# Block 2's output projection with its operands prepared up to 28 steps ahead, and half of the first row half's transposes moved among products of the feed forward

## The chip, the cores and the metric

The kernel runs on one core of a Trainium2 chip. The metric is the device time of one launch in microseconds (us), as the median of several runs. A profile of one execution gives, for each engine, what it ran and what it waited for: TensorE (PE, and PEld for its weight loads), VectorE (DVE), ScalarE (ACT), GpSimd (POOL) and SyncE (SP), whose queue issues the transfers.

## What is computed

Two transformer blocks on one sequence of 1024 rows and 1024 columns, in float32. The first is an attention and pooling mixer. The second, in which the change lies, ends like this (cut):

```python
    merged = g_a * (o_a @ w_branch_a[l]) + g_b * (o_b @ w_branch_b[l])
    x = x + merged @ w_out[l]                              # output projection
    h2 = rms_norm(x, norm2[l])
    x = x + jnp.square(jax.nn.relu(h2 @ w_up[l])) @ w_down[l]   # feed forward, 4096 wide
return rms_norm(x, final_norm)
```

## The kernel before, in words

Every float32 operand of a matmul is split into a high part (a cast on ScalarE, `hi`, L109, to the reduced type fp32r) and a low part (operand minus high part, `lo`, L112, on VectorE or GpSimd). One product of two operands is then three matmuls: high by high, high by low, low by high. All matmuls of this part have a weight tile of 128 x 128 and 512 columns.

The output projection, the up and the down projection are multiplied by a scheme of seven products in place of eight (halves of rows, of columns and of the inner dimension are added and subtracted first). `ORDER` = 1, 6, 7, 4, 2, 5, 3 is their order in the output projection. A product of it is 48 matmuls: 4 tiles t of rows, 4 pieces q of the inner dimension, 3 matmuls each.

**Merge.** `merge` (L1487) is the stretch before: for j = 0 to 7 it multiplies by the branch weights and gathers into `gl`. From j = 4 on, `m_sums` (L1476) forms on VectorE the sums of the merged halves that the projection needs (tiles `ms` and `gl`).

**Operands of the projection.** The object `FO` of class `Feed` holds a list of 72 steps, written by `row_steps` (L845): differences of weight tiles on VectorE (`comb`, L834: tiles `cb` and `wr`, L838) and splits (`split`, L812: a cast `fh`; its low part `fl` is issued with the next step; of 14 low parts 5 go to VectorE, 9 to GpSimd). Product 1 needs the first 8 steps, product 6 the next 20, product 7 another 8, product 4 another 12, products 2, 5 and 3 8 each. A step is issued in one of two ways. `Stream.tick` issues one whenever the program's own clock `e.t` (a sum of model costs over the matmuls issued so far) has moved on by `gap` and the position lies below a goal; `need` issues at once what a product wants and sets the goal `ahead` steps further. `merge` sets the goal by `FO.ahead(8 * (j - 5))`, `row_prod` (L873) by its argument 16. `F` is the same kind of object for the up projection.

**Order of other work.** `e.at(dt, fn)` puts work on a heap, due `dt` ns of program time later. Each engine runs its own instructions strictly in the order in which the program issued them, so these dues decide who stands behind whom.

**Rows.** When a tile of a product is complete, `out2_gather` (L1551) adds it to the residual row tile (`x`, L1554, VectorE). For the last four products it also takes the sum of squares (`junk`, L404, ScalarE); when both column halves are there, `f3` adds them on GpSimd (L1563), takes the inverse root there (`ry`, L117 and L118), scales the row on VectorE (`xs`, two of 512 columns, L1567) and stores `x`. Rows t = 0 to 3 are finished by product 3, rows 4 to 7 by product 5. Only six row tiles exist, so rows 6 and 7 are held back until the first half's transposes are issued.

**Transposes.** `prep0` (L1668) transposes rows 0 to 3 in eight groups of four (`tp`, L104, into one bank); ScalarE copies each out with its gain twice (`hh` L1677 and `hr` L1678) and VectorE forms the low part (`hl`, L1679). `prep1` (L1688) does the same for rows 4 to 7 in four groups of eight, with sums and differences of the two halves (`hr`, L1700 and L1710) and their splits. `interleave` (L958) runs the one generator within the other: `prep0` inside `out2` (L1532), a group every second step after a set time, and at the end of `out2` whatever is left of it at once; `prep1` inside `up_first` (L1776), a group every fourth step.

**Feed forward.** `up_first` runs 21 products of 12 matmuls: product 1 for q = 0, 1, 2, then 2, 4, 5, 6, 7, 3, each for the three q. The first two need rows 0 to 3 alone, in two inner halves ("11" and "12"); product 4 is the first to need rows 4 to 7.

## Time and profile before

| | |
|---|---|
| time, median of 3 runs | 1864.5 us (1864.38 to 1864.9) |
| the profiled execution | 1863.2 us, span 1861.5 us, mean granted clock of TensorE 0.989 |
| TensorE busy | 1802.8 us, 97% of the span |
| VectorE, ScalarE, GpSimd busy | 61%, 52%, 39% |
| share of the chain that ended last | TensorE 86%, VectorE 6%, ScalarE 3%, GpSimd 2%, DMA 1% |

The span is the time from the first to the last profiled event; the execution's time is 1.7 us longer. Busy shares are means over the whole span. The granted clock is a share of TensorE's full speed; matmuls are pipelined, so a busy row may overlap the next one.

### The profile page before, as it was taken

To read this page: it belongs to the slowest core of one execution; us is meant where nothing else is said; L and a number is where in the kernel's file an instruction comes from. 1 tells how busy PE (TensorE), PEld (TensorE's weight loads), DVE (VectorE), ACT (ScalarE), POOL (GpSimd) and SP (SyncE) were. 2 spreads that over 40 slices of the span, in tenths; PEclk is the share of its full clock that TensorE was granted. 3 is DMA by queue.
4 is the path that set the end of the run, shared out by engine and by line. 5 is a ranking of instruction groups with operands and counts; after the bars stand their busy time and mean duration, and the time that the engine had idled before them with its cause. 6 is when DMAs were issued, how large, how long until landed. Compare 5 with 4: busy or idle time off the path is not lost.

```text
span 1861.5 us, 25745 instructions
## 1 busy us (share of the span) xinstructions
PE 1802.8 (97%) x8957; PEld 1513.3 (81%) x8957; DVE 1132.7 (61%) x2081; ACT 962.3 (52%) x1979; POOL 733.7 (39%) x704
## 2 busy tenths in 40 slices
PE   7999999999999999999999999779999998999998
PEld 6888878898898898889888887558888876888886
DVE  6578783645454556655675485576443347766785
ACT  6455453447656667554565214465555554352444
POOL 4123242512212212212111425556544445775873
PEclk9999999999999999999999999889999999999999
DMA  7101132314222212120213923203635368444522
GB/s 203 34 24 35 35 114 69 125 35 92 80 46 85 76 39 60 57 71 26 63 38 107 300 68 119 75 11 128 218 127 183 126 240 303 158 151 138 170 85 91
DMA packets 189187, 195.69 MB, mean 105 GB/s; under 512 B 16944, under 2 KB 124160, under 8 KB 189056
## 3 DMA queue, kind: packets, MB, share of 16 engines
q1 hardware_dynamic: 189056, 194.04, 33.1%
q8 instruction: 70, 1.15, 0.3%
q14 instruction: 61, 0.50, 0.1%
HBM read 141.52 MB, written 54.04 MB: 105 GB/s over the span
## 4 chain that ended last, share of the span: by engine, by line
PE 86%; DVE 6%; issue 3%; ACT 3%; POOL 2%; DMA 1%; POOLq 0%; SPq 0%; ACTq 0%; DVEq 0%
PE mm L99 37%; PE mmmm L99 14%; PE mmT L99 9%; PE mmO L99 7%; PE mmo L99 5%; PE tp L104 4%; PE S L99 4%; PE O L99 4%; POOL fl L112 1%; DVE wr L838 1%; DVE s L1055 1%; ACT junk L404 1%; POOL ry L118 0%; DMA ha<-hid_d 0%; DVE sb L665 0%
## 5 line engine op out<-in xcount | busy, mean ns | idle before, releaser
L112 POOL TENSOR_TENSOR wl<-wr,wh 128x512 fp32r<-128x512 f32 x148 | 198.5, 1347 | 561.7 <-ACT wh L109 320.5
L99 PE MATMUL mm<-hh,wh 128*128 128x512 f32 (+1 forms) x792 | 313.8, 396 | 0.0
L99 PE MATMUL mm<-hl,wh 128*128 128x512 f32 (+1 forms) x792 | 310.1, 392 | 1.1 <-DVE hl L940 1.1
L99 PE MATMUL mm<-hh,wl 128*128 128x512 f32 (+1 forms) x792 | 309.5, 391 | 0.0
L112 POOL TENSOR_TENSOR fl<-wr,fh 128x512 fp32r<-128x512 f32 x161 | 228.7, 1434 | 146.4 <-ACT fh L109 122.1
L109 ACT CAST fh<-wr 128x512 fp32r<-128x512 f32 x216 | 130.4, 617 | 222.0 <-DVE wr L838 170.1
L656 ACT ACTIVATE sb<-sb,nm 128x128 f32<-128x128 f32 (+2 forms) x192 | 125.7, 655 | 149.4 <-DVE nm L650 99.0
L99 PEld LDWEIGHTS mm<-hh,wl 128*128 128x128 f32 x792 | 149.8, 189 | 32.5
L99 PEld LDWEIGHTS mm<-hl,wh 128*128 128x128 f32 x792 | 150.2, 190 | 26.1 <-DVE hl L940 1.6
L99 PEld LDWEIGHTS mm<-hh,wh 128*128 128x128 f32 x792 | 150.2, 190 | 25.3
L112 DVE TENSOR_TENSOR ptl<-tp,pth 128x512 fp32r<-128x512 f32 (+2 forms) x176 | 113.5, 646 | 79.8 <-ACT pth L109 75.8
L112 POOL TENSOR_TENSOR fl<-ha,fh 128x512 fp32r<-128x512 f32 x80 | 122.0, 1542 | 48.9 <-ACT fh L109 35.8
L109 ACT CAST pth<-tp 128x512 fp32r<-128x512 f32 (+2 forms) x176 | 96.4, 548 | 74.0 <-PE tp L104 69.8
L665 DVE TENSOR_SCALAR sb<-sb,rc 128x128 f32<-128x128 f32 (+2 forms) x192 | 97.6, 508 | 6.7
L104 PE MATMUL tp<-ident,sb 128*128 128x128 f32 x648 | 99.7, 272 | 1.3 <-DVE ptl L112 1.0
L109 ACT CAST wh<-wr 128x512 fp32r<-128x512 f32 x148 | 89.9, 617 | 20.7 <-DMA wr<-in_w_branch_a 16.1
L104 PEld LDWEIGHTS tp<-ident,sb 128*128 128x128 f32 x648 | 80.5, 140 | 22.9 <-DVE ptl L112 1.8
L838 DVE TENSOR_TENSOR wr<-wr 128x512 f32<-128x512 f32 x108 | 95.0, 880 | 1.6
L99 PE MATMUL O<-pth,v 128*128 128x256 f32 (+3 forms) x264 | 93.2, 361 | 0.0
L99 PE MATMUL mmmm<-fh 128*128 128x512 f32 x212 | 83.4, 393 | 6.7 <-ACT fh L109 6.7
L99 PE MATMUL mmmm<-fl,fh 128*128 128x512 f32 x212 | 83.8, 395 | 2.4 <-POOL fl L112 1.8
L99 PE MATMUL mmmm<-fh,fl 128*128 128x512 f32 x212 | 83.0, 391 | 0.0
(319 smaller groups left out, 4586.0 us busy)
## 6 DMA issues: line engine op xcount, KB each, us to landing
wr<-in_w_in SPq DMA_DIRECT2D x116, 256.0 KB, 3.4
ha<-hid_d SPq DMA_DIRECT2D x112, 256.0 KB, 3.7
wr<-in_w_up SPq DMA_DIRECT2D x64, 256.0 KB, 3.8
hid_d<-hc SPq DMA_DIRECT2D x64, 256.0 KB, 2.7
wr<-in_w_down SPq DMA_DIRECT2D x64, 256.0 KB, 4.2
hid_d<-pk SPq DMA_DIRECT2D x45, 256.0 KB, 3.8
wr<-in_w_out SPq DMA_DIRECT2D x32, 256.0 KB, 5.0
x_d<-x SPq DMA_DIRECT2D x32, 256.0 KB, 2.1
```

What stands on the lines that cost most here:

```text
L99: self.nc.tensor.matmul(out=out, lhsT=lhsT, rhs=rhs, start=start, stop=stop, skip_group_check=skip)
L104: self.nc.tensor.transpose(out, in_, ident)
L109: self.nc.scalar.copy(out, in_)
L112: (eng or self.nc.vector).tensor_tensor(out=out, in0=in0, in1=hi.bitcast(F32), op=ALU.subtract)
L404: ACT.activation(j[:, 0:n], src, AF.Square, accum_out=acc)
L656: ACT.activation(d[:, 0:w], d[:, 0:w], AF.Exp, bias=nm, scale=-1.0, accum_out=g.sm[:, j:j + 1])
L665: V.tensor_scalar(out=d[:, 0:w], in0=d[:, 0:w], scalar1=g.rc[:, j:j + 1], scalar2=None, op0=ALU.mult)
L838: eng.tensor_tensor(out=self.raw[dst], in0=self.raw[x], in1=self.raw[y], op=op)
L1055: V.tensor_tensor(out=nxt[:, a0:1040], in0=cur[:, a0:1040], in1=cur[:, a0 - n:1040 - n], op=ALU.add)
```

## The change

The preparation of the projection's operands is issued further ahead: a step every 800 ns of program time instead of 1500, a goal of 8 and then 20 steps in the last two rounds of the merge (before 8 and 16), and 20 or 28 steps ahead of a product (before 16). The feed forward's own first steps are asked for once, 8 of them with product 3 (n = 6), before 6 with product 5 and 12 with product 3. The root of a row becomes a piece of work of its own, `f2`, due 1650 ns after the gather; scaling and store, `f3`, are due at 3000. Of `prep0`'s eight groups only four have to be issued by the end of `out2`. The other four, and then `prep1`, run inside `up_first`, by the generator `preps`, which takes a turn every second step.

```diff
-    def interleave(main, side, start, every):
+    def interleave(main, side, start, every, rest=False):
...
         if side is not None:
+            if rest:
+                return side
             run(side)
...
-    FO.look = 8
+    FO.look, FO.s.gap = 8, 800.0
...
             if j > 5:
-                FO.ahead(8 * (j - 5))
+                FO.ahead(8 if j == 6 else 20)
...
                 F.load(0, n - 3)
-                F.ahead(6 * (n - 4))
+            if n == 6:
+                F.ahead(8)
             e.wide = i not in (5, 3)
-            yield from row_prod(FO, i, range(4), 16, out2_gather)
+            yield from row_prod(FO, i, range(4), 20 if n < 2 else 28, out2_gather)
...
             def f3():
-                POOL.tensor_tensor(out=ss[:, 2:3], in0=ss[:, 0:1], in1=ss[:, 1:2], op=ALU.add)
-                r = e.rstd(ss[:, 2:3])
                 xs = e.row("xs")
...
+            rs = []
+
+            def f2():
+                POOL.tensor_tensor(out=ss[:, 2:3], in0=ss[:, 0:1], in1=ss[:, 1:2], op=ALU.add)
+                rs.append(e.rstd(ss[:, 2:3]))
+            e.at(1650, f2, ("rs2", t))
+
+            def f23():
+                e.need(("rs2", t))
+                f3()
             if t < 6 or rows_free:
-                e.at(1650, f3, ("xs2", t))
+                e.at(3000, f23, ("xs2", t))
             else:
-                held.append((f3, ("xs2", t)))
-            xs2_t[t] = e.t + 4450
+                held.append((f23, ("xs2", t)))
+            xs2_t[t] = e.t + 4900
...
+        assert ("12", 3) in HA
         for q in qs:
...
-    interleave(out2(), prep0, lambda: xs2_t.get(3), 2)
-    interleave(up_first(), prep1, lambda: xs2_t[7], 4)
+    first = interleave(out2(), prep0, lambda: xs2_t.get(3), 2, True)
+
+    def preps():
+        if first is not None:
+            yield from first
+        for _ in range(200):
+            if e.t >= xs2_t[7]:
+                break
+            yield
+        for _ in prep1():
+            yield
+            yield
+    while first is not None and ("11", 3) not in HA:
+        next(first)
+    interleave(up_first(), preps, None, 2)
```

In the orders below a row is a line of the program, the operation, and result and operand by their names; of the changed kernel the lines are some higher (L1559 is the gather L1554, L1570 is `xs` L1567, L1692 is `hl` L1679, L1713 is L1700).

**First place.** VectorE's queue behind the last `m_sums`, at the first product of the projection. Before:

```order
L1483 TENSOR_TENSOR ms<-gl,ms 128x512
L838 TENSOR_TENSOR wr<-wr 128x512
L1554 SCALAR_TENSOR_TENSOR x_11512<-mmmm,x_11512 128x512
L1554 SCALAR_TENSOR_TENSOR x_11514<-mmO,x_11514 128x512
L838 TENSOR_TENSOR cb<-wr 128x512
L112 TENSOR_TENSOR fl<-wr,fh 128x512
L1554 SCALAR_TENSOR_TENSOR x_11516<-mmT,x_11516 128x512
L838 TENSOR_TENSOR wr<-wr 128x512 x2
L838 TENSOR_TENSOR cb<-wr 128x512
L112 TENSOR_TENSOR fl<-wr,fh 128x512
L838 TENSOR_TENSOR wr<-wr 128x512 x2
L1554 SCALAR_TENSOR_TENSOR x_11518<-mmmm,x_11518 128x512
```

After:

```order
L1487 TENSOR_TENSOR ms<-gl,ms 128x512
L838 TENSOR_TENSOR cb<-wr 128x512
L112 TENSOR_TENSOR fl<-wr,fh 128x512
L1559 SCALAR_TENSOR_TENSOR x_11525<-mmmm,x_11525 128x512
L838 TENSOR_TENSOR wr<-wr 128x512 x2
L1559 SCALAR_TENSOR_TENSOR x_11527<-mmO,x_11527 128x512
L1559 SCALAR_TENSOR_TENSOR x_11529<-mmT,x_11529 128x512
L1559 SCALAR_TENSOR_TENSOR x_11531<-mmmm,x_11531 128x512
L112 TENSOR_TENSOR fl<-ms,fh 128x512
L1559 SCALAR_TENSOR_TENSOR x_11617<-mmmm,x_11617 128x512
```

The last `wr` pair (the two differences for q = 3) stands two rows behind the first `fl` instead of at the end of the piece; the differences and low parts that stood between have moved up into the merge.

**Second place.** VectorE's queue at product 5's gathers, where rows are finished. Before:

```order
L1554 SCALAR_TENSOR_TENSOR x_11711<-mmo,x_11711 128x512
L1567 TENSOR_SCALAR xs<-x_11797,ry 128x512
L1567 TENSOR_SCALAR xs<-x_11711,ry 128x512
L112 TENSOR_TENSOR fl<-ms,fh 128x512
L1554 SCALAR_TENSOR_TENSOR x_11713<-mm,x_11713 128x512
L838 TENSOR_TENSOR cb<-wr 128x512
L1567 TENSOR_SCALAR xs<-x_11799,ry 128x512
L1567 TENSOR_SCALAR xs<-x_11713,ry 128x512
L838 TENSOR_TENSOR wr<-wr 128x512
L1554 SCALAR_TENSOR_TENSOR x_11715<-mmo,x_11715 128x512
L112 TENSOR_TENSOR fl<-wr,fh 128x512
L1567 TENSOR_SCALAR xs<-x_11801,ry 128x512
```

After:

```order
L1559 SCALAR_TENSOR_TENSOR x_11728<-mmo,x_11728 128x512
L1559 SCALAR_TENSOR_TENSOR x_11730<-mm,x_11730 128x512
L1570 TENSOR_SCALAR xs<-x_11829,ry 128x512
L1570 TENSOR_SCALAR xs<-x_11728,ry 128x512
L1559 SCALAR_TENSOR_TENSOR x_11732<-mmo,x_11732 128x512
L1570 TENSOR_SCALAR xs<-x_11831,ry 128x512
L1570 TENSOR_SCALAR xs<-x_11730,ry 128x512
L1559 SCALAR_TENSOR_TENSOR x_11734<-mm,x_11734 128x512
L1570 TENSOR_SCALAR xs<-x_11833,ry 128x512
L1570 TENSOR_SCALAR xs<-x_11732,ry 128x512
L1559 SCALAR_TENSOR_TENSOR x_11617<-mmo,x_11617 128x512
L1570 TENSOR_SCALAR xs<-x_11835,ry 128x512
```

The low parts `fl` of product 3's operands, and the differences `cb` and `wr` of the up projection, no longer stand between the gathers and the scalings `xs`.

**Third place.** TensorE at the end of product 3 and the beginning of `up_first`; `tp` are transposes, four to a group of the first half and eight to one of the second; `mm<-fh` are products of the projection, `mmo<-hh` of the feed forward. Before:

```order
L104 MATMUL tp<-ident,xs 128x128 x4
L99 MATMUL mm<-fh 128x512
L99 MATMUL mm<-fl,fh 128x512
L99 MATMUL mm<-fh,fl 128x512
L104 MATMUL tp<-ident,xs 128x128 x16
L99 MATMUL mmo<-hh,fh 128x512
L99 MATMUL mmo<-hl,fh 128x512
L99 MATMUL mmo<-hh,fl 128x512
L99 MATMUL mmo<-hh,fh 128x512
L99 MATMUL mmo<-hl,fh 128x512
```

After, from the seventh group's products on:

```order
L99 MATMUL mm<-hl,fh 128x512
L99 MATMUL mm<-hh,fl 128x512
L104 MATMUL tp<-ident,xs 128x128 x4
L99 MATMUL mmo<-hh,fh 128x512
L99 MATMUL mmo<-hl,fh 128x512
L99 MATMUL mmo<-hh,fl 128x512
L99 MATMUL mmo<-hh,fh 128x512
L99 MATMUL mmo<-hl,fh 128x512
L99 MATMUL mmo<-hh,fl 128x512
L104 MATMUL tp<-ident,xs 128x128 x8
L99 MATMUL mmo<-hh,fh 128x512
L99 MATMUL mmo<-hl,fh 128x512
```

Before, the last four groups stood together (`x16`), and the first transposes of the second half 24 matmuls behind them (row 5646 of the program). Now six matmuls of the feed forward stand between one group and the next, and six between the first half's last group and the second half's first eight transposes.

VectorE there, after:

```order
L1692 SCALAR_TENSOR_TENSOR hl<-tp,gains,hh 128x512
L838 TENSOR_TENSOR wr<-wr 128x512
L1559 SCALAR_TENSOR_TENSOR x_11623<-mm,x_11623 128x512
L1692 SCALAR_TENSOR_TENSOR hl<-tp,gains,hh 128x512 x5
L1570 TENSOR_SCALAR xs<-x_11529,ry 128x512
L1570 TENSOR_SCALAR xs<-x_11621,ry 128x512
L1570 TENSOR_SCALAR xs<-x_11531,ry 128x512
L1570 TENSOR_SCALAR xs<-x_11623,ry 128x512
L1713 SCALAR_TENSOR_TENSOR hr<-tp,gains,hr 128x512
L838 TENSOR_TENSOR cb<-wr 128x512
```

The scalings `xs` of rows 6 and 7 stand behind all `hl` of the first half, and the first work on the second half's transposes (`hr<-tp`) behind them; before, the scalings of row 6 stood ahead of the last two `hl`.

ScalarE a little later, at the second half's third and fourth transposes (`hh<-tp`, `hh<-S`), after:

```order
L109 CAST hh<-hr 128x512 x2
L1714 ACTIVATE hh<-tp,gains 128x512
L1715 ACTIVATE hr<-tp,gains 128x512
L109 CAST hh<-hr 128x512
L109 CAST fh<-wr 128x512
L1750 ACTIVATE hc<-mm 128x512
L1751 ACTIVATE hc<-hc 128x512
L109 CAST hh<-hr 128x512 x2
L1714 ACTIVATE hh<-S,gains 128x512
L1715 ACTIVATE hr<-S,gains 128x512
L109 CAST hh<-hr 128x512
L109 CAST fh<-wr 128x512
```

The first `fh<-wr` is the cast of the weight of q = 2 for product 2; it stands behind the copies of the third eight transposes, as it did before, and the next `fh<-wr`, for product 4, behind those of the fourth with one cast between, where before there were five operations.

## Rows read from the trace of the kernel before

**Rows 1.** The page: busy time and share of each engine with its number of instructions; the shares of the chain that ended last; one group of instructions (its busy time and the mean ns of one); one group of transfers (size, us from issue to landing).

```profile
PE 1802.8 (97%) x8957; PEld 1513.3 (81%) x8957; DVE 1132.7 (61%) x2081; ACT 962.3 (52%) x1979; POOL 733.7 (39%) x704
PE 86%; DVE 6%; issue 3%; ACT 3%; POOL 2%; DMA 1%; POOLq 0%; SPq 0%; ACTq 0%; DVEq 0%
L112 POOL TENSOR_TENSOR fl<-wr,fh 128x512 fp32r<-128x512 f32 x161 | 228.7, 1434 | 146.4 <-ACT fh L109 122.1
wr<-in_w_up SPq DMA_DIRECT2D x64, 256.0 KB, 3.8
```

**Rows 2.** The table by stages: from and to (us of the span), length, then busy us of PE, PEld, DVE, ACT and POOL with their instructions, the granted clock, the DMA share, GB/s. The stages are product 1; product 6; products 7, 4 and 2; products 5 and 3 with four groups of transposes; the other four groups; `up_first`; all that follows.

```profile
1107.50:1118.40 10.90, 10.90 (x49) 9.03 (x49) 10.80 (x16) 1.14 (x2) 1.87 (x2) 1.00 0.29 95
1118.40:1136.10 17.70, 14.62 (x50) 10.79 (x50) 10.36 (x12) 6.44 (x12) 10.47 (x8) 0.81 0.30 103
1136.10:1170.00 33.90, 33.19 (x146) 26.89 (x145) 18.88 (x24) 16.75 (x37) 16.44 (x13) 1.00 0.35 101
1170.00:1210.20 40.20, 28.93 (x113) 21.07 (x111) 24.50 (x33) 16.07 (x37) 21.68 (x33) 0.83 0.24 89
1210.20:1219.60 9.40, 3.34 (x17) 2.31 (x17) 3.67 (x6) 5.30 (x10) 1.29 (x4) 0.78 0.11 42
1219.60:1289.80 70.20, 64.71 (x286) 52.42 (x285) 47.31 (x56) 41.97 (x75) 46.13 (x32) 0.96 0.12 35
1289.80:1861.50 571.70, 556.56 (x2437) 458.20 (x2436) 345.96 (x426) 276.99 (x500) 340.27 (x255) 0.99 0.50 168
```

**Rows 3.** What TensorE waited for from 1107.5 to 1290 us, the largest: waiting operation, releaser, us in total, times, longest us.

```profile
PE tp L104 <- DVE hl L1679: 9.5, 5, 3.4
```

**Rows 4.** The same view from 1289.8 us to the end, the two largest.

```profile
PE mmmm L99 <- ACT fh L109: 4.2, 2, 2.4
PE mmT L99 <- DVE pk L1764: 1.4, 1, 1.4
```

**Rows 5.** Two rows of the chain that ended last (start us, us, what) and two of the list of TensorE's instructions (start us, us, engine, line, operation, result and operands, shape, number).

```profile
1126.02 4.76 PE mmO L99 x12
1257.26 2.72 PE mmo L99 x12
...
1226.46 1.03 PE L104 MATMUL tp<-ident,xs 128*128 128x128 f32 x8
1227.25 0.48 PE L99 MATMUL mmo<-hh,fh 128*128 128x512 f32 x1
```

**Rows 6.** The list of instructions around product 6 (in brackets the idle time before and what ended it): VectorE's last start after an idle time and, 33 operations later, the last pair of differences; behind it ScalarE, TensorE and GpSimd.

```profile
1096.88 0.69 DVE L1513 SCALAR_TENSOR_TENSOR gl<-gl,mm 128x512 f32<-128x512 f32 x1 [1.43 <-PE mm L99]
...
1120.11 2.58 DVE L838 TENSOR_TENSOR wr<-wr 128x512 f32<-128x512 f32 x2
1122.78 0.62 ACT L109 CAST fh<-wr 128x512 fp32r<-128x512 f32 x1 [2.79 <-DVE wr L838]
1123.45 0.80 PE L99 MATMUL mmmm<-fh 128*128 128x512 f32 x1 [2.46 <-ACT fh L109]
1123.47 1.28 POOL L112 TENSOR_TENSOR fl<-wr,fh 128x512 fp32r<-128x512 f32 x1 [2.13 <-ACT fh L109]
```

**Rows 7.** The list of instructions in product 3 and behind it: a row's sum of squares, its sum on GpSimd, its scaling; a low part behind it on VectorE; the matmul that waited for that; two later scalings.

```profile
1184.07 0.60 ACT L404 ACTIVATE junk<-x 128x512 f32<-128x512 f32 x1 [6.93 <-DVE x L1554]
1184.87 0.20 POOL L1563 TENSOR_TENSOR ss<-ss 128x1 f32<-128x1 f32 x1 [2.04 <-ACT junk L404]
1186.02 1.87 DVE L1567 TENSOR_SCALAR xs<-x,ry 128x512 f32<-128x512 f32 x2 [1.44 <-POOL ry L118]
1189.02 0.68 DVE L112 TENSOR_TENSOR fl<-wr,fh 128x512 fp32r<-128x512 f32 x1
1189.75 0.80 PE L99 MATMUL mmo<-fl,fh 128*128 128x512 f32 x1 [3.60 <-DVE fl L112]
...
1221.98 0.87 DVE L1567 TENSOR_SCALAR xs<-x,ry 128x512 f32<-128x512 f32 x2
```

**Rows 8.** The list of instructions at one group of transposes: ScalarE's two copies and VectorE's low part.

```profile
1209.27 0.67 ACT L1677 ACTIVATE hh<-tp,gains 128x512 fp32r<-128x512 f32 x1
1209.84 0.68 ACT L1678 ACTIVATE hr<-tp,gains 128x512 f32<-128x512 f32 x1
1210.55 0.75 DVE L1679 SCALAR_TENSOR_TENSOR hl<-tp,gains,hh 128x512 fp32r<-128x512 f32 x1 [1.63 <-ACT hr L1678]
```

**Rows 9.** The list of TensorE's instructions in `up_first`: its two waits of more than 2 us.

```profile
1242.48 0.50 PE L99 MATMUL mmo<-hh,fl 128*128 128x512 f32 x1 [3.47 <-POOL fl L112]
1254.70 0.50 PE L99 MATMUL mm<-hh,fl 128*128 128x512 f32 x1 [2.02 <-POOL fl L112]
```

**Rows 10.** Three groups of VectorE's instructions in `up_first` (shape, number, busy us, mean ns of one, idle us before them), and rows of the list at one meeting of VectorE and GpSimd.

```profile
L112 DVE TENSOR_TENSOR hl<-hr,hh 128x512 fp32r<-128x512 f32 x4 | 5.1, 1286 | 0.0
L1803 DVE TENSOR_TENSOR u<-pk,u 128x512 f32<-128x512 f32 x3 | 3.0, 1017 | 0.1
L1700 DVE SCALAR_TENSOR_TENSOR hr<-tp,gains,hr 128x512 f32<-128x512 f32 x6 | 4.3, 741 | 5.3 <-ACT hr L1702 5.3
...
1247.83 1.75 POOL L112 TENSOR_TENSOR fl<-wr,fh 128x512 fp32r<-128x512 f32 x1
1248.34 1.78 DVE L112 TENSOR_TENSOR hl<-hr,hh 128x512 fp32r<-128x512 f32 x1
1249.53 3.44 POOL L112 TENSOR_TENSOR hl<-hr,hh 128x512 fp32r<-128x512 f32 x2
```

More of the change, by code (lines that the diff above doesn't have):

```diff
@@ L956, in g_Tq @@
             yield 327.0
-    def interleave(main, side, start, every):
+    def interleave(main, side, start, every, rest=False):
         side, n = side(), 0
+        if start is None:
+            start = lambda: 0.0
         for _ in main:
@@ L1562, in f3 @@
             def f3():
-                POOL.tensor_tensor(out=ss[:, 2:3], in0=ss[:, 0:1], in1=ss[:, 1:2], op=ALU.add)
-                r = e.rstd(ss[:, 2:3])
                 xs = e.row("xs")
                 for j in range(2):
-                    V.tensor_scalar(out=xs[:, 512 * j:512 * j + 512], in0=x2[t, j], scalar1=r, scalar2=None, op0=ALU.mult)
+                    V.tensor_scalar(out=xs[:, 512 * j:512 * j + 512], in0=x2[t, j], scalar1=rs[0], scalar2=None, op0=ALU.mult)
                 xs2[t] = xs
```

## The prediction

> **What bounds the kernel now.** I read the page first: TensorE is busy 97% of the span and 86% of the chain that ended last is its own [rows 1]. So only two things can be won: time in which TensorE waits, and time in which it runs at the lower clock. The table by stages shows where both lie: in the 182.3 us from the first product of block 2's output projection to the last of `up_first` [rows 2]. Of the 571.7 us after that 15.1 are without a matmul, at places that the change does not touch; the two longest groups of waits in them are 4.2 and 1.4 us [rows 2, 4].
>
> What would those 182.3 us take without a wait and at the full clock? Twelve matmuls of 512 columns take 2.72 us [rows 5]. The stretch holds 7 products of 48 and 21 of 12, 588 matmuls: 49 x 2.72 = 133.3 us. Eight transposes at the full clock occupy the 0.79 us from their first to the next matmul [rows 5]; there are 64, so 6.4 us. Together 139.7, so **42.6 us are lost**. By stages [rows 2]: product 6 takes 17.7 us where 48 matmuls need 10.9 (6.8 lost); products 7, 4 and 2 lose 33.9 - 32.6 = 1.3; products 5 and 3 with the first four groups of transposes lose 40.2 - 21.8 - 1.6 = 16.8; the other four groups, alone, 9.4 - 1.6 = 7.8; `up_first` 70.2 - 57.1 - 3.2 = 9.9. TensorE is idle for 26.6 of them (each stage's length less its busy time: 3.1, 0.7, 11.3, 6.1 and 5.5), 9.5 of these behind the low parts `hl` of the transposed rows [rows 2, 3]. The other 16.0 are the clock: right after a wait twelve matmuls take 4.76 us [rows 5], and the granted clock of these stages is 0.78 to 0.96 where it is 1.00 before them [rows 2]. It falls to its lower level (1.2 of 2.4 GHz) after a cluster of waits. The one wait of 2.02 us at 1254.70 in `up_first` was not followed by that: from 1257.26 twelve matmuls took 2.72 [rows 5, 9].
>
> **Product 6: operands too late.** VectorE has been full since 1096.9 (10.80 of product 1's 10.90) [rows 2, 6] when it finishes the last two differences for q = 3 at 1122.69; ScalarE's cast, and behind it TensorE and GpSimd's low part, follow at once [rows 6]. The first place of the order shows what moves: the last pair now stands five places behind `m_sums`, before twelve, and two earlier low parts go to where VectorE idled. Counted from 1096.88 (its last idle moment), 31 operations are ahead of that end instead of 34. At 0.76 us each (25.8 us for 34) the pair ends 2.3 us earlier, at 1120.4; the cast ends 0.62 later, at 1121.0, the low part 1.28 after it, at 1122.3 [rows 6]. TensorE wants the two at 1120.5 and 1120.9 (product 6 starts at 1118.4, nine matmuls at 0.227 ahead). Half a microsecond is left for the first, 0.8 for the second: I take 1.0 for both, as the idle moment filled counts a little too. Bounds: 0 and the old 6.8.
>
> **Products 7 to 3: preparation out of the way.** At 0.8 us a step with up to 28 ahead, all casts and low parts of product 3 stand ahead of product 5's row sums (second place: no `fl` among the `xs` any more). They must be done in time: 26 low parts fall to GpSimd, 1.43 us each on the mean [rows 1], 37 us from 1121, so by 1158; product 3 starts at 1107.5 + 6 x 10.9 + 1 = 1174. The cover is 16 us; without it product 3 waits as it did. The old waits were a lockstep [rows 7]: VectorE stood before each `xs` for GpSimd's root, with product 3's low parts queued behind it, and TensorE behind these. That goes, also because the root is now issued 1.35 us of program time ahead of the scaling.
>
> The transposes need the last row's `xs`. After product 5's fourth gather (0.69, as the merge's in [rows 6]) come the sum of squares (0.8 from its start to GpSimd's), the root (1.15 from there to `xs`) and `xs` [rows 7], which stands behind the gather of product 3's first group at 2.7 + 0.7: done 4.3 us into product 3. The first group of transposes stands 27 matmuls, 6.1 us, into it: no wait. Of the 9.5 us on `hl` [rows 3] I leave 0.7 (bounds 0 and 3.0), since an `hl` still stands behind `xs` and differences. The last four groups lie six matmuls apart (1.36 us); ScalarE's two copies of each start 0.57 apart and VectorE's `hl` takes 0.75 [rows 8], which fits in 1.36 + 0.4. So the 7.8 us of the lonely groups go, but for that 0.7.
>
> **`up_first`: something comes back.** Three waits are new or moved (third place).
> First, the second half's transposes begin six matmuls after the last group of the first half, and need the rows 6 and 7. These find a buffer only when that group has been read, and stand in VectorE's queue behind all its `hl`. Chain: `hh` 0.57, a copy of a product 0.5, `hr` 0.57, `hl` 0.7, four `xs` of 0.44 [rows 7, 8], hand-overs 0.2: 4.3 us. Cover: six matmuls and two or three transposes, 1.8. Wait 2.5 (1.8 to 3.5). Before, 24 matmuls lay between.
> Second, the cast of the weight of q = 2, second product, stands behind the two copies (`hh`, `hr`) that wait for the third pair of transposes, in a queue of five casts and copies of 0.55 (a start to the next start [rows 8]), with 0.5 of backlog; less a cover of six matmuls (1.4) that is 1.9. Then GpSimd's 1.28 [rows 6] less two matmuls, 0.8: 2.7, taken as 3.0 for what else GpSimd has queued. It replaces the old 3.47 [rows 9].
> Third, the last pair of transposes stands behind that wait now (before, ahead of it), and product 4 of q = 0 needs its low part `hl`: the weight's cast and low part wait again, 1.0 + 1.5; then `hl`, which stands on VectorE behind two products with the gain and three operations of two SBUF inputs, 3 x 0.74 + 3 x 1.1 = 5.5 after `hr`, with a backlog of two more at 0.74, less the 2.5 just waited and eight matmuls (1.8): 2.7; then the next weight, 0.8. Together 6.0 (3 to 9), where before 2.0 were waited [rows 9, 10].
>
> How long are those two-input operations? The means there run from 1.02 (`u`) to 1.29 (`hl`); I take 1.1. GpSimd and VectorE alternate: VectorE's `hl` of 1248.34 began while GpSimd's `fl` ran, took 1.78 and ended at 1250.12, 0.5 us after that `fl`; GpSimd's next two took 3.44 [rows 10].
> The Trainium skill ("SBUF — State Buffer", section "Who interferes with whom") says that a VectorE instruction with two SBUF inputs and a GpSimd instruction that reads SBUF exclude each other, the later one blocked to the end. These rows agree. If every one of the three met a GpSimd operation, the third wait would be 2.0 longer, and the sum would give 1842 instead of 1840.
>
> **The clock.** 16.0 us went with 26.6 of waits, 0.6 for each. All three new waits, 11.5 us, lie in a cluster; 0.6 x 11.5 = 6.9, and since the 2.0 us wait cost none, I take 5.0 (0 to 10).
>
> **Sum.** Lost after: 1.0 + 0.7 + 2.5 + 3.0 + 6.0 + 5.0 = 18.2 us, against 42.6: 24.4 less. The profiled execution took 1863.2 us (span 1861.5), so 1838.8; the median of the runs is 1.3 above it: **1840**. The rest of the edit I cost at nothing: `F.ahead(8)` instead of 6 and 12 issues the same casts, covered by product 3's full rate; the reordered stores and loads on the SP queue (row 0's store ahead of the third group of `w_up`) move that group's issue behind product 5's first gather, about 1166, and at 3.8 us to landing [rows 1] it is there long before its cast at about 1175; if it were late, the sums of squares behind that cast would be too.
>
> **Rivals.**
> - *Nothing comes back.* ScalarE and VectorE run ahead and only product 6 and the transposes cost: 42.6 - 3 = 39.6 less, 1825. Against it: the chain for rows 6 and 7 has no cover. Chance 0.07.
> - *More comes back.* The lock between VectorE and GpSimd takes its full turns (third wait 11) and the clock stays low from the second half's transposes to product 4 (12): lost 30, gain 12.5, 1852. For it: GpSimd is busy 46 of the 70 us there [rows 2]. Chance 0.19. This is where the skill's rule cited above would lead if each meeting cost a turn.
> - *Nothing changes.* VectorE is the bound as before, so product 6 waits on, and GpSimd's queue holds `up_first` until the old time. It would have to take 24 us of early start; the first operation of that queue hangs on the transposes, which come earlier by all that is won before. Chance 0.03: 1864.
> - *Slower.* In `up_first`, where waits now come in short succession, the clock does not rise again. A matmul then costs 2.04 / 12 = 0.17 us more [rows 5]. Slower needs over 42.6 + 3.7 lost, so 33 us by the clock beside 13.2 of waits: 194 matmuls, 16 of the 21 groups. For it: the waits lie 7 us apart at first; against it: after the first cluster the clock was 1.00 for the whole next stage [rows 2]. Price at 18 groups: 36.7 + 13.2 = 49.9 lost, 1872. Chance 0.05.
> - The forecast itself: 0.66.
>
> **Numbers.** The terms' bounds give 6.6 lost at the least (1828) and about 35 at the most (1857). The range leaves out the two outer cases and half of "more comes back": **1831 to 1852**. A change under 0.2% (3.7 us) is about what a measurement of this kernel cannot tell from none. Faster by more: 0.66 + 0.07 + 0.19, with a part of the third lost, 0.92; within: 0.03; slower: 0.05.
>
> **What would show it.** Right: no wait of TensorE over 1.5 us from 1107 to 1187; no `xs` of VectorE waiting for a root by more than 0.5 us while a low part is queued; product 3 in 12.5 us; four groups of transposes between matmuls with under 1 us of waits; then three waits, on `xs`, on `fl` and on `fl` or `hl`, and `up_first` in 72 to 80 us instead of 70.2. Wrong: a wait on ScalarE at product 6 as long as before; a granted clock under 0.8 through `up_first`; or a new wait in the merge, where the differences now stand ahead of gathers that free the product banks.

## The result, and the profile after

The changed kernel takes 1840.41 us (median of 4 runs, 1839.55 to 1840.87) where the kernel before, beside it, takes 1864.67: a ratio of 0.9869 (95% interval 0.9852 to 0.9887). The profiled execution took 1840.53 us with a span of 1838.8, 22.7 us less than that of before. The page of the changed kernel, by engines and along the chain:

```profile
PE 1796.4 (98%) x8957; PEld 1510.1 (82%) x8957; DVE 1133.5 (62%) x2081; ACT 962.4 (52%) x1979; POOL 740.1 (40%) x704
PE 89%; DVE 5%; ACT 2%; issue 2%; POOL 1%; DMA 0%; POOLq 0%; SPq 0%; DVEq 0%; ACTq 0%
```

The work is the same, matmul for matmul [rows 1]; less of it is waited for. The table by stages of the changed kernel (columns as in [rows 2]): product 1; product 6; products 7, 4 and 2; products 5 and 3 with four groups of transposes; `up_first` with the other four; the rest.

```profile
1107.87:1118.80 10.93, 10.93 (x49) 8.93 (x48) 10.79 (x15) 2.39 (x4) 3.02 (x2) 1.00 0.53 163
1118.80:1132.50 13.70, 11.54 (x50) 9.04 (x49) 12.01 (x16) 6.52 (x13) 10.37 (x8) 1.00 0.28 97
1132.50:1165.20 32.70, 32.70 (x146) 27.05 (x146) 23.29 (x26) 20.37 (x43) 30.01 (x20) 1.00 0.32 98
1165.20:1189.96 24.76, 24.01 (x114) 19.41 (x112) 15.91 (x25) 11.42 (x27) 12.48 (x25) 1.00 0.53 187
1189.96:1266.80 76.84, 69.28 (x302) 54.76 (x300) 53.16 (x65) 47.40 (x85) 47.60 (x37) 0.93 0.13 39
1266.80:1838.80 572.00, 556.81 (x2437) 458.31 (x2436) 345.89 (x426) 276.91 (x500) 340.55 (x255) 0.99 0.51 168
```

From product 1 to the last of `up_first` it is 158.9 us instead of 182.3: 23.4 less, and outside nothing moved by more than 0.4. Against the same 139.7 us of full work 19.2 are still lost: 10.5 of idle time (lengths less busy times: 2.2, 0.8 and 7.6) and 8.7 by slower work. The stage of products 5 and 3, 40.2 + 9.4 us before, is 24.8 now, 24.8 less. Product 6 adds 4.0 to this and products 7, 4 and 2 add 1.2; `up_first` gives 6.6 back, 1.6 of them the 16 transposes that moved into it (at the 0.79 us of eight [rows 5]). What TensorE waits for in this stretch, all that is over 0.6 us in total:

```profile
PE mmo L99 <- ACT fh L109: 2.5, 1, 2.5
PE tp L104 <- DVE xs L1570: 1.9, 2, 1.4
PE mmo L99 <- POOL fl L112: 1.5, 2, 1.0
PE mmmm L99 <- DVE x L1559: 1.3, 1, 1.3
PE mm L99 <- POOL fl L112: 0.8, 1, 0.8
PE mmmm L99 <- POOL fl L112: 0.8, 1, 0.8
PE mm L99 <- DVE hl L1713: 0.8, 1, 0.8
PE tp L104 <- DVE hl L1692: 0.7, 1, 0.7
```

The 9.5 us on `hl` of the first half [rows 3] are 0.7 now, and no low part of the projection is waited for behind product 6.

### The profile page after: what moved, and what is told of

The parts are those of the page before. It is cut to its first block, busy times and chain, and to the rows that moved or that the text cites. A ratio compares the mean times of both kernels' runs of the same rounds, so it can differ in the third digit from the quotient of the medians.

```text
span 1838.8 us, 25751 instructions
## 1 busy us (share of the span) xinstructions
PE 1796.4 (98%) x8957; PEld 1510.1 (82%) x8957; DVE 1133.5 (62%) x2081; ACT 962.4 (52%) x1979; POOL 740.1 (40%) x704
## 4 chain that ended last, share of the span: by engine, by line
PE 89%; DVE 5%; ACT 2%; issue 2%; POOL 1%; DMA 0%; POOLq 0%; SPq 0%; DVEq 0%; ACTq 0%
PE mm L99 39%; PE mmmm L99 15%; PE mmT L99 10%; PE mmO L99 7%; PE mmo L99 6%; PE tp L104 4%; PE S L99 4%; PE O L99 4%; DVE wr L838 1%; DVE s L1059 1%; POOL fl L112 0%; ACT junk L404 0%; POOL ry L118 0%; ACT sb L656 0%; DVE sb L665 0%
## 5 line engine op out<-in xcount | busy, mean ns | idle before, releaser
L109 ACT CAST pth<-tp 128x512 fp32r<-128x512 f32 (+2 forms) x176 | 96.3, 548 | 74.4 <-PE tp L104 70.2
```

The lines of the kernel that those rows point to most:

```text
L109: self.nc.scalar.copy(out, in_)
```

## The experiments

Each run stood beside the kernel before on the same chip (medians of before: 1864.2, 1863.7, 1864.0 and 1863.5 us). Intervals of a ratio are some 0.0015 to either side, about 2.8 us, so differences of one or two us between runs are read from the stages of the profiles.

**One part alone.** Preparation alone: the changed kernel with the root and the transposes as before.

```diff
-            e.at(1650, f2, ("rs2", t))
...
             def f23():
-                e.need(("rs2", t))
+                f2()
                 f3()
...
-                e.at(3000, f23, ("xs2", t))
+                e.at(1650, f23, ("xs2", t))
...
-            xs2_t[t] = e.t + 4900
+            xs2_t[t] = e.t + 4450
...
-    first = interleave(out2(), prep0, lambda: xs2_t.get(3), 2, True)
...
-    interleave(up_first(), preps, None, 2)
+    interleave(out2(), prep0, lambda: xs2_t.get(3), 2)
+    interleave(up_first(), prep1, lambda: xs2_t[7], 4)
```

> The change's preparation alone: step gap 800, goals of 8 and 20 in the merge, 20 and 28 ahead of a product, the feed forward's first steps asked for once; root and scaling together and the transposes as in the kernel before. Theory (the terms of the sum are separate): product 6 waits about 2.2 us as in the changed kernel, products 5 and 3 lose 2 to 5 instead of 16.8, the four lonely groups keep their 7.8 lost and up_first its 9.9. Lost about 23 of 139.7 + 23, so 20 us less than before: 1845 (1841 to 1849). Rival (the parts work only together, since the scalings that wait for a root still hold the low parts of the transposes): products 5 and 3 lose 10 or more, 1852 or above.

Measured: 1854.98 us, ratio 0.9948 (0.9933 to 0.9963). The rival's figures came: products 5 and 3 lose 10.4 us (33.8 from 1165.50 to the first of the four lonely groups at 1199.27, less 23.4 of full work), and the time lies above 1852. Its reason, that the parts work only together, does not hold: below, two of them add up. Move alone: the changed kernel with the root as above and the preparation as before.

```diff
-    FO.look, FO.s.gap = 8, 800.0
+    FO.look = 8
...
-                FO.ahead(8 if j == 6 else 20)
+                FO.ahead(8 * (j - 5))
...
-            if n == 6:
-                F.ahead(8)
+                F.ahead(6 * (n - 4))
...
-            yield from row_prod(FO, i, range(4), 20 if n < 2 else 28, out2_gather)
+            yield from row_prod(FO, i, range(4), 16, out2_gather)
```

> The move of the transposes alone: four groups of the first half among products of the feed forward, preparation and root as in the kernel before. Theory: the 7.8 us of the lonely groups go, products 6, 5 and 3 lose what they lost before (6.8 and about 16.8), and up_first loses 5 to 10 more than before's 9.9, as in the changed kernel (19 us less 7 of other stages): 1862 (1858 to 1865). Rival (nothing comes back in up_first when it starts late enough for its weights): 1857 or below.

Measured: 1860.03 us, ratio 0.9976 (0.9966 to 0.9986), in the theory's range. Root alone: the kernel before with the change's `f2` and `f23` (its diff from `def f3` to `xs2_t`) and nothing else.

> The kernel before with the split of root and scaling alone (root due 1650 ns after the gather, scaling 3000, transposes from 4900). Theory A (the lockstep is VectorE standing before each scaling for GpSimd's root, so the split ends it by itself): products 5 and 3 lose 16.8 less some 9, the 9.5 us that the changed kernel lost when the split was undone: 1855 (1852 to 1858). Theory B (the split works only with the low parts of product 3 out of VectorE's and GpSimd's queues, that is with the preparation): within 3 us of before, 1861 to 1865.

Measured: 1855.52 us, ratio 0.9957 (0.9940 to 0.9973): theory A. The stage of products 5 and 3 to the first product of the feed forward, 49.6 us in the kernel before, with the preparation alone, with the move alone and with the root alone:

```profile
1165.50:1207.30 41.80, 28.59 (x129) 22.94 (x128) 21.79 (x32) 16.28 (x35) 12.81 (x28) 0.89 0.35 120
```

```profile
1168.70:1210.30 41.60, 29.86 (x114) 22.19 (x113) 25.26 (x34) 17.43 (x38) 21.96 (x33) 0.84 0.24 89
```

```profile
1170.20:1212.00 41.80, 30.04 (x130) 22.74 (x128) 28.93 (x39) 21.32 (x46) 26.44 (x36) 0.85 0.25 95
```

Each part by itself takes 8 us out of it; of the move's 8.0, 1.6 are 16 transposes that only change the stage. `up_first`, 70.2 us before, takes 73.7, 76.0 and 71.1 in these runs. The parts cure different waits. VectorE's wait for roots in this stage (us in total, times, longest us), before and with the root alone:

```profile
DVE xs L1567 <- POOL ry L118: 12.6, 6, 4.8
DVE xs L1565 <- POOL ry L118: 2.9, 2, 2.5
```

With the preparation alone it is still 11.6, with preparation and root there is none. TensorE's wait for low parts `fl` on VectorE, 6.4 us before in this stage, is gone with the preparation alone, and is 4.8 with the root alone and 6.7 with the move alone.

**Two parts.** Preparation and move, the changed kernel with only the root as before (the first lines of the first diff above):

> The changed kernel with a row's root and scaling issued together again, 1650 ns after the gather, and the transposes' start at 4450. Theory: with no low part queued behind them, scalings that wait for a root hold up only the gathers and the transposes' low parts, 0.7 to 1.2 us for each of the last rows: 1 to 3 us more than the changed kernel, 1841.5 to 1843.5. Rival (the split of the root carries the end of the lockstep): 1845 or above. Other rival (it does nothing): 1840.4 within 0.5.

Measured: 1849.86 us, ratio 0.9920 (0.9906 to 0.9935). The split is worth 9.5 us beside the two others: the first rival. Preparation and root, the changed kernel with only the transposes as before (the last lines of that diff):

> Preparation and split root together, the transposes as in the kernel before. Each alone took 8 us out of the stage of products 5 and 3 with the first half's transposes (49.6 us), as did the move alone, and all three together 24.8. Theory (three separate causes, so any two add up): that stage 33 to 34.5 us, and the whole 1864 - 9.2 - 8.2 = 1846.5 (1844.5 to 1848.5). Rival (preparation and split cure the same lockstep, so the second adds little): stage 38 or more, 1851 or above.

Measured: 1846.48 us, ratio 0.9906 (0.9891 to 0.9921): theory. The gain, 17.5 us, is the sum of the two (9.2 + 8.2), closer than the intervals could show. The same stage, of preparation and move, then of preparation and root:

```profile
1164.80:1199.30 34.50, 26.66 (x114) 21.56 (x113) 18.76 (x27) 12.38 (x28) 11.92 (x25) 0.85 0.40 138
```

```profile
1164.90:1199.40 34.50, 27.53 (x129) 21.57 (x128) 20.14 (x32) 16.41 (x35) 13.62 (x28) 0.90 0.41 145
```

From 49.6 over 41.7 and 34.5 to 24.8: three causes, each of 7 to 10 us in every order that was run (move and root without the preparation were not run together). What is left of the lockstep without the split is to be seen on VectorE. Its longest wait in that stage with preparation and move but no split, and its list of instructions there:

```profile
DVE xs L1570 <- POOL ry L118: 11.6, 6, 2.0
```

```profile
1170.44 0.88 DVE L1570 TENSOR_SCALAR xs<-x,ry 128x512 f32<-128x512 f32 x2 [2.04 <-POOL ry L118]
1171.23 0.69 DVE L1559 SCALAR_TENSOR_TENSOR x<-mm,x 128x512 f32<-128x512 f32 x1
1173.96 0.88 DVE L1570 TENSOR_SCALAR xs<-x,ry 128x512 f32<-128x512 f32 x2 [2.04 <-POOL ry L118]
...
1177.48 1.90 DVE L1570 TENSOR_SCALAR xs<-x,ry 128x512 f32<-128x512 f32 x2 [2.04 <-POOL ry L118]
1179.31 0.68 DVE L1559 SCALAR_TENSOR_TENSOR x<-mm,x 128x512 f32<-128x512 f32 x1
1182.02 1.87 DVE L1570 TENSOR_SCALAR xs<-x,ry 128x512 f32<-128x512 f32 x2 [2.04 <-POOL ry L118]
```

No low part of the projection stands here any more, and the loop is still closed: a gather, then two scalings that wait 2.04 us for the square sum and the root of the same row, and only behind them the gather of the next row, from which its root follows. A row takes 3.5 us (1170.44, 1173.96, 1177.48), and 4.5 (1177.48, 1182.02) once GpSimd forms low parts of the feed forward while the scaling runs, so that this takes 1.90 instead of 0.88. TensorE finishes a row in 2.72; VectorE falls behind, and at the end the transposes wait (6.6 us on one `hl`). With the split the changed kernel has:

```profile
1176.26 0.69 DVE L1559 SCALAR_TENSOR_TENSOR x<-mm,x 128x512 f32<-128x512 f32 x1 [1.24 <-PE mm L99]
1176.86 1.31 DVE L1570 TENSOR_SCALAR xs<-x,ry 128x512 f32<-128x512 f32 x2
1178.98 0.69 DVE L1559 SCALAR_TENSOR_TENSOR x<-mmo,x 128x512 f32<-128x512 f32 x1 [0.80 <-PE mmo L99]
1179.59 1.50 DVE L1570 TENSOR_SCALAR xs<-x,ry 128x512 f32<-128x512 f32 x2
```

The scaling behind a gather is now that of the row before; a row takes 2.72 us, and what VectorE waits for is TensorE.

**What `up_first` waits for.** The changed kernel with more of the feed forward's steps in the idle time of product 3:

```diff
-                F.ahead(8)
+                F.ahead(18)
```

> The changed kernel with 18 instead of 8 of the feed forward's first steps asked for with product 3: eight more weight differences of VectorE stand among the transposes of the first half, where it is idle for 3.0 of 7.4 us, instead of among those of the second half. Theory (VectorE's queue is what up_first waits for): the waits on the weight of q = 2, 3.06 us, and at product 4, 2.63, fall to 2.5 together, and with them most of the lower clock of 1214 to 1232 (5.4 us): 1840.4 - 3.2 - 3 = 1834 (1831 to 1837). Rival (the chain of copies, casts and transposes sets these waits, not the differences): 1839 to 1841. Rival on the other side: the low parts of the first half come later and hold the transposes among the products, 1842 or above.

Measured: 1836.01 us, ratio 0.9846 (0.9832 to 0.9861), in the theory's range, though the waits fall to 3.3 us and not 2.5. `up_first` takes 72.9 us instead of 76.8; the waits on the weight of q = 2 are gone, and those at product 4 are one:

```profile
PE mm L99 <- DVE hl L1713: 3.3, 1, 3.3
PE tp L104 <- DVE xs L1570: 2.4, 2, 1.9
```

The weight's cast now stands ahead of all copies of the second half, and VectorE has none of the feed forward's differences between 1211.06 and 1222, where the changed kernel has six (1212.13 to 1222.84); which of the two did it, this run does not tell. With the steps asked for as in the kernel before (for n = 4 to 6, so 6 with product 5 and 12 with product 3):

```diff
-            if n == 6:
-                F.ahead(8)
+                F.ahead(6 * (n - 4))
```

> The changed kernel with the feed forward's first steps asked for as before: 6 with product 5 and 12 with product 3 instead of 8 with product 3. The prediction cost this edit at nothing; the preparation alone made up_first 3.5 us longer, and 18 steps took 3.9 us out of it. Theory (the change's 8 steps instead of 12 are what up_first pays for): up_first 73 to 75.5 us instead of 76.8, 1838.5 (1837 to 1839.5). Rival (8 or 12 make no difference, only 18 reach past product 2's weights): 76.3 to 77.3 and 1840.4 within 0.7. Rival on the other side (steps during product 5 hold up its row scalings on VectorE and GpSimd): 1841.5 or above.

Measured: 1839.61 us, ratio 0.9870 (0.9854 to 0.9887), `up_first` 77.6 us: nearest to the first rival. 8 or 12 make no difference that the runs can tell, and the theory fell. Why the preparation alone lengthens `up_first` by 3.5 us stays open. Then, on top of 18 steps, the sums `s4` later:

```diff
-            e.at(12000 + 1000 * k, lambda r12=r12, s2=s2: V.tensor_tensor(out=r12, in0=r12, in1=s2, op=SUB))
-            asplit("s4", k, r12, 14000 + 1000 * k, POOL)
+            e.at(24000 + 1000 * k, lambda r12=r12, s2=s2: V.tensor_tensor(out=r12, in0=r12, in1=s2, op=SUB))
+            asplit("s4", k, r12, 26000 + 1000 * k, POOL)
```

> The run with 18 steps asked for early, and besides the sums s4 (r12 less s2 and their split, which only product 3 of the feed forward needs) due 24000 instead of 12000 ns after their transposes, so that they don't stand ahead of the last low part of rows 4 to 7 on VectorE. Theory (what is left of the third wait, 3.3 us on that low part, is the place in VectorE's queue: one s4 of 1.6 us and its meetings with GpSimd): the wait falls to 1.5 or less and the slow 12 matmuls behind it with it, 1836.0 - 3 = 1833 (1831.5 to 1834.5). Rival (the low part waits for its transposes and copies): 1835.5 to 1836.5. Rival on the other side: s4 now collides with the totals of product 6 and 7, 1837 or above.

Measured: 1834.21 us, ratio 0.9845 (0.9831 to 0.9860). The time lies in the theory's range, but its ratio is that of the run without this edit. The wait on `hl` is 1.8 instead of 3.3, not under 1.5, and 1.6 us come back behind `up_first`, where a product waits for VectorE's totals: `up_first` takes 71.6 us. On top of 18 steps, the last rows' scalings earlier:

```diff
             e.at(800, lambda ps=ps, h=h, l=l, g=g: V.scalar_tensor_tensor(
...
+            if k == KT - 1:
+                for t in range(4):
+                    xs2.pop(t)
+                rows_free.append(True)
+                for n, (f, tag) in enumerate(held):
+                    e.at(50 + 300 * n, f, tag)
             yield 436.0
```

> The run with 18 steps asked for early, and besides the scalings of rows 6 and 7 released with the last group of the first half's transposes, ahead of that group's low part instead of behind it. Theory (the first of the three new waits, 2.4 us there, is the scalings' place behind the last low part, which waits 1.5 us for ScalarE's copy): it falls by 1.3 to 2.4, and the slow 12 matmuls behind it (1.9 us more) may go too: 1833.5 (1832 to 1835). Rival (the scalings wait for the transposes to read the old rows, so nothing changes): 1835.5 to 1836.5.

Measured: 1836.02 us, ratio 0.9855 (0.9840 to 0.9869): nothing, and not for the rival's reason. The scalings began 2.2 us sooner (1197.82 instead of 1200.02; 0.4 waited for them instead of 2.4), but the transposes then waited 1.7 for the last group's `hl`, whose bank they need.

**Product 6.** The changed kernel with the merge's preparation begun a round earlier:

```diff
-            if j > 5:
-                FO.ahead(8 if j == 6 else 20)
+            if j > 4:
+                FO.ahead((8, 14, 24)[j - 5])
```

> The changed kernel with the merge's preparation begun one round earlier: goals of 8, 14 and 24 steps at j = 5, 6, 7 instead of none, 8 and 20. Product 6's 2.2 us (1.3 on the gather of product 1's first tile, 0.8 on a weight's low part) are what VectorE's queue leaves. Theory: the gathers stand right behind the last sums and the weights are ready, product 6 loses under 0.5: 1840.4 - 2 = 1838.4 (1837.9 to 1838.9). Rival (VectorE has too little room in the merge, so the merge's own gathers come late and TensorE waits there): 1840 or above.

Measured: 1839.24 us, ratio 0.9869 (0.9855 to 0.9884), the ratio of the changed kernel, and a time between theory and rival. Products 1 and 6 take 21.9 us instead of 24.6, without a wait; `up_first`, which begins earlier, takes 78.2 instead of 76.8, at the weights of product 2 and behind it. By the profile 1.4 us are won, too few for the ratio.

**Together.** 18 steps, late `s4` and the earlier merge:

> The run with 18 steps and the late s4, with the merge's preparation begun one round earlier as in the run that did that alone. There product 6 gave back 2.7 us and up_first took 1.4 of it, at the weight of q = 2 and its neighbours, waits that 18 steps remove. Theory: the two gains add up, 1834.2 - 2.5 = 1831.7 (1830.5 to 1833). Rival (up_first is bound by the chain of the second half's transposes, so what comes earlier is waited for there): 1833.5 to 1834.5.

Measured: 1832.53 us, ratio 0.9831 (0.9817 to 0.9846), as the theory has it: product 6 keeps its 10.9 us and `up_first` takes 71.5. And with the earlier scalings and ScalarE's second copy right behind the first:

```diff
-            e.at(650, lambda ps=ps, r=r, g=g: ACT.activation(r, ps, AF.Copy, scale=g))
+            e.at(150, lambda ps=ps, r=r, g=g: ACT.activation(r, ps, AF.Copy, scale=g))
```

> The run before last in this list (18 steps, late s4, merge earlier), and besides rows 6 and 7 scaled ahead of the last low part of the first half, and ScalarE's second copy of each group (hr) due right behind the first instead of 500 ns later, so that no copy of a product and no cast stands between them. Theory (the low part that took the scalings' place as the first wait in up_first stood for that copy, which came 1.0 us after the first because two operations lay between): the wait at the second half's first transposes, 2.1 to 2.4 us, falls to 1.0 to 1.4, 1 us less than the other run (0.5 to 2.5 less). Rival (the chain transposes, copy, copy, low part, transposes is as long as the six matmuls allow): within 0.4 of the other run.

Measured: 1830.08 us, ratio 0.9819 (0.9802 to 0.9835), some 10 us below the changed kernel. The wait at the second half's transposes is 0.38 + 0.73 us, as the theory has it, and `up_first` is at the full clock:

```profile
1188.10:1256.90 68.80, 64.13 (x302) 51.79 (x300) 53.30 (x65) 46.67 (x85) 48.77 (x38) 1.00 0.13 40
```

The last two lie 2.5 us apart with intervals that overlap; the stages (71.5 and 68.8) say the same as the medians.

## Why the prediction was right, and where not

The time (1840, and 1840.4 measured) and the sum of what is lost (18.2, and 19.2) came out. That they came so close is in part luck: three terms are off by 1.2, 3.4 and 3.7 us, not all to the same side. The terms, against the changed kernel's rows:

| | predicted lost | measured |
|---|---|---|
| product 6 | 1.0 (0 to 6.8) | 2.2 |
| transposes behind `hl`, products 5 and 3 | 0.7 (0 to 3.0) | 0.7 |
| first wait in `up_first`, on `xs` | 2.5 (1.8 to 3.5) | 1.9 |
| second, the weight of q = 2 | 3.0 | 3.1 |
| third, at product 4 | 6.0 (3 to 9) | 2.6 |
| the clock and slower work | 5.0 (0 to 10) | 8.7 |

Of its signs of being right one failed: product 3 takes 13.9 us (1176.06 to 1189.96) and not 12.5, 0.7 of it the wait on `hl`, the rest in small pieces around the transposes. Its least loss, 6.6, does not come out of its own bounds: with 3.0 for the second wait, for which it gives no bound, they make 7.8. Nothing hangs on that.

**Product 6: the right cause of the old wait, the wrong next one.** The weights' last pair comes earlier, by 1.0 us and not by the 2.3 of the forecast (an end at 1121.66 instead of 1122.69). But product 6 adds to product 1's banks, and the first of these was not yet gathered:

```profile
1117.88 1.78 DVE L112 TENSOR_TENSOR fl<-wr,fh 128x512 fp32r<-128x512 f32 x1
1119.59 0.68 DVE L1559 SCALAR_TENSOR_TENSOR x<-mmmm,x 128x512 f32<-128x512 f32 x1
1120.19 1.47 DVE L838 TENSOR_TENSOR wr<-wr 128x512 f32<-128x512 f32 x2
1120.41 0.47 PE L99 MATMUL mmmm<-fh 128*128 128x512 f32 x1 [1.34 <-DVE x L1559]
```

The gather stood ahead of the low part in the order of before and stands behind it now. The prediction named this (differences ahead of gathers that free the banks) for the merge, among what would make it wrong, and not for product 6, and gave it no price; it is 1.3 of the 2.2.

**Products 5 and 3: the size right, the reason half.** The prediction put the end of the lockstep down to the low parts that leave VectorE's queue, and mentioned the root's split behind an "also", without a price. In this stage the runs give the two the same price (8 us each alone; 9.5 in the time for the split beside the others). Had the split been left out, the same reasoning would have forecast no lockstep, and been 9.5 us too low. The step that failed is the reading of [rows 7]: a scaling that waits 1.44 us for its own root, with the next gather behind it, is a loop of its own, with or without low parts in VectorE's queue. In the run without the split it takes 3.5 us a row, and 4.5 beside GpSimd's low parts, both more than TensorE's 2.72. The cover of product 3's operands held, with 11.6 us instead of 16: VectorE's last low part ended at 1164.46, GpSimd's before it, and product 3 begins at 1176.1:

```profile
1160.91 3.00 POOL L112 TENSOR_TENSOR fl<-ms,fh 128x512 fp32r<-128x512 f32 x2
1163.26 1.20 DVE L112 TENSOR_TENSOR fl<-wr,fh 128x512 fp32r<-128x512 f32 x1
```

**The lonely groups** behaved as said: eight groups among matmuls cost 0.7 us of waits in all.

**The second wait: right size, wrong chain.** The cast of that weight came at 1212.51, as ScalarE had stood idle for VectorE, not for the transposes:

```profile
1207.92 1.71 DVE L838 TENSOR_TENSOR wr<-wr 128x512 f32<-128x512 f32 x1
1209.55 0.74 DVE L1713 SCALAR_TENSOR_TENSOR hr<-S,gains,hr 128x512 f32<-128x512 f32 x1
1210.32 0.62 ACT L109 CAST hh<-hr 128x512 fp32r<-128x512 f32 x1 [0.93 <-DVE hr L1713]
1212.51 0.63 ACT L109 CAST fh<-wr 128x512 fp32r<-128x512 f32 x1
1213.18 0.50 PE L99 MATMUL mmo<-hh,fh 128*128 128x512 f32 x1 [2.53 <-ACT fh L109]
```

The third eight transposes had ended at 1209.27, before the casts that stood ahead of their copies were through. The difference `wr` of the feed forward that took 1.71 us met GpSimd's low part of 1207.80 to 1209.08; with 18 steps, where both it and the cast stand earlier, the wait is gone.

**The third wait and the clock: two terms off in opposite directions.** `hl` came 5.5 us behind ScalarE's copy (an end at 1219.69, and one at 1225.20), which is what the prediction sums for it and the five operations before it; the backlog of two more, 1.5, that it adds was not there:

```profile
1219.01 0.68 ACT L1715 ACTIVATE hr<-S,gains 128x512 f32<-128x512 f32 x1
1224.46 0.74 DVE L1713 SCALAR_TENSOR_TENSOR hl<-S,gains,hh 128x512 fp32r<-128x512 f32 x1
```

But the clock fell, twice between 1214 and 1232: behind the second wait, and behind the last piece of the third. The table by stages has the stretch, and the two pieces:

```profile
1214.00:1232.00 18.00, 14.85 (x46) 10.82 (x46) 17.61 (x19) 10.74 (x20) 14.69 (x10) 0.72 0.00 1
1214.50:1220.30 5.80, 5.76 (x18) 4.74 (x18) 5.80 (x8) 2.80 (x6) 3.33 (x2) 0.50 0.01 3
1227.40:1230.60 3.20, 3.18 (x8) 2.50 (x9) 2.92 (x3) 1.28 (x3) 3.20 (x2) 0.50 0.00 0
```

From 1220.8 to 1227.3 the granted clock is 1.00. 38 matmuls and eight transposes, 9.4 us at the full clock, took 14.85: 5.4 us more. Some 3.2 of these lie in the first piece (1214.54 to 1220.76, where ten matmuls and the eight transposes need 3.06). It ran while VectorE and GpSimd caught up, so that less was left to wait for at product 4 (2.6 instead of 6.0). The second piece comes behind that wait and saved nothing of it. How much of the missing 3.4 is the slow piece, and how much the backlog that was not there, no run separates. The sum of both terms, 11.0, was measured as 11.3. It seems that waits priced at the full clock and the clock priced by itself count the same stretch twice when both are large; no run held the clock up to show it. The other 3.3 us of slower work lie in pieces of under 1.2 around the waits and the transposes; what makes them up was not settled.

Of the rivals, "more comes back" asked for full turns of the lock and a clock that stays low to product 4; the lock took turns in places (`wr` of 1207.92 in 1.71 us), and the low clock came in two pieces, the last inside product 4, but neither reached its price. The other three are excluded: `up_first` began 29.6 us earlier and ended 23.0 earlier, so something came back, but not all, and the time fell.

## What to carry to other kernels

When a wait closes a loop (a scaling that waits for its own row's root, with the next row's first step queued behind it), count its period against the rate of the engine that feeds it; taking other work out of the queue shortens it, letting the queue run one row behind opens it. Fill an idle stretch of the second engine with the work that its next crowded stretch holds, and look for who frees the buffer that the first engine wants next: an operand that is ready gains nothing more while the bank is full.

## What the runs showed of the hardware

The clock cost no fixed share of the waits, where the prediction takes 0.6 us of clock for each us of waiting. In the changed kernel TensorE idled 1.34 and 0.82 us at product 6 with ten matmuls between, and the stage's clock was 1.00; before, it idled 2.46 us there [rows 6] and 0.56 more at 1124.80, and twelve matmuls a little behind took 4.76 us instead of 2.72 [rows 5]. At the transposes of the second half, with 18 steps, the list of TensorE and the chain have:

```profile
1200.56 0.33 PE L104 MATMUL tp<-ident,xs 128*128 128x128 f32 x1 [1.93 <-DVE xs L1570]
1201.35 0.77 PE L104 MATMUL tp<-ident,xs 128*128 128x128 f32 x5 [0.46 <-DVE xs L1570]
```

```profile
1202.11 4.34 PE mmo L99 x12
```

and in the changed kernel, at the same place, 1.42 and 0.46 us of waiting:

```profile
1200.49 0.33 PE L104 MATMUL tp<-ident,xs 128*128 128x128 f32 x1 [1.42 <-DVE xs L1570]
```

From the first of the twelve matmuls to the next transposes it is 4.42 us with 18 steps (1201.87 to 1206.29) and 2.82 in the changed kernel (1201.80 to 1204.62). Half a microsecond more of waiting came with 1.6 us of slower matmuls.

VectorE's operations with two SBUF inputs took up to 1.8 us singly where they met GpSimd, 0.68 where they did not; those with one SBUF input and one from PSUM did not change. One of each against the same engine, in the changed kernel:

```profile
1207.80 1.28 POOL L112 TENSOR_TENSOR hl<-hr,hh 128x512 fp32r<-128x512 f32 x1 [0.38 <-ACT hh L109]
1214.44 1.74 POOL L112 TENSOR_TENSOR hl<-hr,hh 128x512 fp32r<-128x512 f32 x1
1214.96 0.74 DVE L1713 SCALAR_TENSOR_TENSOR hr<-tp,gains,hr 128x512 f32<-128x512 f32 x1
```

`wr` of 1207.92 (above) ended 0.55 us after the first of these, in 1.71; the second ran over the whole of `hr<-tp`, whose 0.74 is that of the others shown. That fits the rule of the Trainium skill that the prediction cites ("SBUF — State Buffer", section "Who interferes with whom"), by which a VectorE instruction with two SBUF inputs contends with GpSimd's reads. But one SBUF input alone is no shelter: the scalings `xs`, which read one tile from SBUF, took 0.88 us for two while GpSimd was idle, and 1.90 where its low part of 1177.41 to 1178.70 ran beside them (the list of the run without the split, above).
